# Sparse down of the second context token block on VectorE, in token-major form

## The chip, the cores and the metric

The kernel runs on 1 core of one Trainium2 chip, which has eight cores. The metric is the device time of one execution in microseconds; the median of the runs is compared. The five engines of the core that the text speaks of are PE (TensorE, products), DVE (VectorE), ACT (ScalarE), POOL (GpSimd, here the issuer of indirect gathers) and SP (SyncE, the issuer of all other transfers). They run side by side and each takes its instructions in the order in which they stand in its queue.

## The reference, cut to what matters

Two layers of a hybrid backbone run over 256 latent tokens (stream X) and 256 context tokens (stream C). Each layer ends with a PEER feed-forward: every token picks 128 experts (8 heads of 16) out of 16384, and each expert is one row of `u_emb` and one row of `v_emb`, 1024 numbers of 4 bytes each.

```
idx = ...                                    # (tokens, 8 heads, 16): the experts of each token
gate = softmax(best_s)
act = gelu(einsum('td,thkd->thk', h, u_emb[idx]))
out = einsum('thk,thkd->td', gate * act, v_emb[idx])     # 128 rows of v_emb, weighted and summed
ctx = ctx + g2c * out                        # in layer 0 alone; layer 1 leaves the context there
```

The change concerns the last sum, for the second 128 of the 256 context tokens in layer 0.

## The kernel before, in words

All 256 latent tokens take the feed-forward in a dense form (generator `dense`, lines 1149 to 1205): all 16384 experts are computed for all tokens and masked. The work goes in 64 steps (`i2`) of two blocks of 128 experts. A step has 48 products for the hidden side (helper `gemm`, lines 371 to 373, tile `pg`) and 48 for the output side (line 1199, tile `acc`). Its weights come as eight tiles `raw` of 256 KB (line 349, five buffers, issued on SP), and each is split into a high part on ACT (line 290, `wh`) and a low part on DVE (line 291, `wl`); a `raw` buffer is free when its low part is done. Two multiplications on DVE (line 1189, `ge`) apply the mask, which comes in tiles `gr` of 512 KB.

The 256 context tokens of layer 0 take it in a sparse form (generator `sparse`, lines 1007 to 1098), in two blocks of 128 tokens, `tb` 0 and 1. Three passes run over 128 positions each:

- `up(tb, p)` gathers, for slot p, one row of `u_emb` per token (tile `u`, 128 x 1024, 512 KB, one row on the partition of its token) and multiplies it with the token's activations `htok` on DVE, with a sum along the row (line 1038, two halves of 512).
- `mid(tb)` turns the sums into weights (gelu times gate) and transposes them on PE, so that each token has its 128 weights in one column `wT`.
- `down(tb, n)` takes one token t. It gathers the 128 rows of `v_emb` of that token (tile `v`, again 128 x 1024; the rows are the token's slots) and lets PE sum them over the partitions: the token's weight column is put into a small band of zeros `wz` (line 1057, once for four tokens), and two products of 32 x 512 (line 1065, each of which shows as two in the trace) add the token's row into the PSUM tiles `pf`.

Pass 0 has `up(0)`, pass 1 `down(0)` and `up(1)` in turns, and pass 2 `down(1)` alone. `fin(tb)` copies `pf` to a tile `f` (line 1071), transposes it by PE (line 1075) and adds it to the context stream (lines 1081 and 1084). Tiles `u`, `v` and `f` share one pool of four buffers of 512 KB, tag `g`.

A list written out by hand (`ORDER`, lines 1207 to 1216) cuts the generators of both streams into pieces, and a scheduler orders the instructions of each engine from it. Through pass 2 the dense steps of X run beside the context's `down(1)`. What comes behind `fin(1)` for the context is its part of layer 1 (a norm, line 314; products, line 367; a triangular solve on DVE, lines 736 and 738, whose results go to products of 32 x 32 at lines 760 and 771), which the latents of layer 1 need.

```
for a in range(3):
    for p in range(P):
        if a:
            down(a - 1, p)
        if a < 2:
            up(a, p)
...
```

Of the kernel before, what the change touches and what calls it, by code (L numbers as in the profile page):

```python
# [15 lines left out]
OP = mybir.AluOpType  # L16
# [153 lines left out]
class Kernel:  # L170
# [836 lines left out]
    def sparse(self, l, st, R):  # L1007
        hts, top = R["htok"], R["top"]
        nc, io, C, m = self.nc, self.io, self.C, self.M[l]
        V, A = nc.vector, nc.scalar  # L1010
        off = lambda ap: bass.IndirectOffsetOnAxis(ap=ap, axis=0)
        sp = self.S("sp", [P, 2, 4, P])
        for tb in range(2):
            ff = self.route(top, tb, "g")
            s, ef = sp[:, tb], self.S("ef", [P, P])
            V.scalar_tensor_tensor(ef.rearrange("p (h k) -> p h k", k=16), ff[:, 0], float(NK), ff[:, 1],
                                   op0=OP.mult, op1=OP.add)
            V.tensor_copy(s[:, 0].bitcast(I32), ef)
            pt = self.PS()
            nc.tensor.transpose(pt[:, :128], ef, C["ident"])  # L1020
            V.tensor_copy(s[:, 1].bitcast(I32), pt[:, :128])
            V.tensor_copy(s[:, 2].rearrange("p (h k) -> p h k", k=16), ff[:, 2])
            yield
        z = self.S("wz", [P, 512])
        nc.gpsimd.memset(z, 0.0)
        idx = lambda tb, i: sp[:, tb, i].bitcast(I32)
        pf = {}
        wT, d2 = [None, None], [None, None]

        def up(tb, p):  # L1030
            if p == 0 and self.DH[tb] == 2:
                d2[tb] = self.S("d2", [P, P])
            u = self.T4("u", tag="g")
            nc.gpsimd.indirect_dma_start(out=u, out_offset=None, in_=io["pu"], in_offset=off(idx(tb, 0)[:, p:p + 1]))  # L1034
            for k in range(self.DH[tb]):
                w = D // self.DH[tb]
                c = slice(w * k, w * k + w)
                V.scalar_tensor_tensor(u[:, c], u[:, c], 1.0, hts[tb][:, c], op0=OP.mult, op1=OP.mult,  # L1038
                                       accum_out=(sp[:, tb, 3] if k == 0 else d2[tb])[:, p:p + 1])

        def mid(tb):
            dots = sp[:, tb, 3]
            if self.DH[tb] == 2:
                V.tensor_tensor(dots, dots, d2[tb], op=OP.add)
            A.activation(dots, dots, AF.Gelu_apprx_tanh)
            V.tensor_tensor(dots, dots, sp[:, tb, 2], op=OP.mult)
            pt = self.PS()
            nc.tensor.transpose(pt[:, :128], dots, C["ident"])
            wT[tb] = self.S("ef", [P, P])
            V.tensor_copy(wT[tb], pt[:, :128])  # L1050
            pf[tb] = [self.PS("pf"), self.PS("pf")]

        def down(tb, n):
            j, g = n // 4, n % 4
            hz = z[:, 256 * (j % 2):256 * (j % 2) + 256]
            if g == 0:
                V.tensor_copy(hz.rearrange("p (g m) -> p g m", g=4)[:, :, 31],
                              wT[tb].rearrange("p (g j) -> p g j", g=4)[:, :, j])
            t = 32 * g + j
            o = 64 * g + 31 - j  # L1060
            v = self.T4("v", tag="g")
            nc.gpsimd.indirect_dma_start(out=v, out_offset=None, in_=io[f"pv{l}"], in_offset=off(idx(tb, 1)[:, t:t + 1]))  # L1062
            for hf in range(2):
                q = 32 * ((g + 2 * hf) % 4)
                nc.tensor.matmul(pf[tb][hf][q:q + 32], hz[:, o:o + 32], v[:, 512 * hf:512 * hf + 512],  # L1065
                                 start=j == 0, stop=j == 31)

        def fin(tb):
            f = self.T4("f", tag="g")
            for hf in range(2):  # L1070
                A.activation(f[:, 512 * hf:512 * hf + 512], pf[tb][hf], AF.Copy)
            for hf in range(2):
                pt = self.PS()
                for c in range(4):
                    nc.tensor.transpose(pt[:, 128 * c:128 * c + 128], f[:, 512 * hf + 128 * c:512 * hf + 128 * c + 128], C["ident"])
                for c in range(4):
                    v = self.xs[st][hf][:, c, 128 * tb:128 * tb + 128]
                    d = pt[:, 128 * c:128 * c + 128]
                    for q in range(2 if hf else 0):
                        i, o = slice(64 * (1 - q), 64 * (1 - q) + 64), slice(64 * q, 64 * q + 64)  # L1080
                        V.scalar_tensor_tensor(v[:, o], d[:, i], m["g2"][:, 4 * hf + c, st:st + 1], v[:, o],
                                               op0=OP.mult, op1=OP.add)
                    if hf == 0:
                        V.scalar_tensor_tensor(v, d, m["g2"][:, c, st:st + 1], v, op0=OP.mult, op1=OP.add)

        for a in range(3):
            for p in range(P):
# [4 lines that stand above are left out]
                if p % 8 == 7:  # L1092
                    yield
            if a:
                fin(a - 1)
            if a < 2:
                mid(a)
            yield
# [178 lines left out]
```

## Time and profile before

| what | value |
|---|---|
| median of 3 runs | 3490.35 us (3487.57 to 3492.45) |
| the profiled execution | 3496.04 us, of which its span is 3494.3 us |
| PE busy | 3315.0 us (95% of the span) |
| DVE, ACT, POOL busy | 2337.6, 1411.2, 553.1 us |
| granted TensorE clock, mean | 0.962 of full |
| bytes moved | 800.48 MB, mean 229 GB/s |
| `down(1)` and its `fin` | about 1620 to 2024 us of the span |

The profile comes from one execution on the chip. Busy time of PE counts pipelined products from start to modelled end, so 95% is not 95% of what PE could compute. "q0 software_dynamic" is the queue of POOL's gathers, "q1 hardware_dynamic" that of SP's transfers; both are served by the same 16 DMA engines.

### The profile page before, as it was taken

What the parts mean: (1) busy time and instruction counts of PE and PEld (TensorE: products, weight loads), DVE (VectorE), ACT (ScalarE), POOL (GpSimd) and SP (SyncE); (2) the same over time, 40 slices, a digit from 0 to 9 for tenths busy, and PEclk for the clock granted to TensorE, in tenths of its full rate; (3) what the DMA queues carried; (4) which work ended last, traced back from release to release, by engine and by line L of the source; (5) the groups of instructions that cost most, each with busy time, mean ns of one, the idle gap of its engine ahead of it and who ended that gap; (6) DMA issues with size and microseconds to landing.
All of it is one profiled execution on the core that took longest, in us unless ns stands there. A gap on an engine that the chain in (4) does not pass through costs nothing.

```text
span 3494.3 us, 69804 instructions
## 1 busy us (share of the span) xinstructions
PE 3315.0 (95%) x26540; PEld 2810.4 (80%) x26540; DVE 2337.6 (67%) x6304; ACT 1411.2 (40%) x2677; POOL 553.1 (16%) x529
## 2 busy tenths in 40 slices
PE   7999989799899879999999999899999999999999
PEld 4797668667667657777777799798889999999999
DVE  4864578777777976565333356877569998755555
ACT  3453133021113433333333354543545666455554
POOL 0000000444343434333333300000000000000000
PEclk9999989879999989999999999899999999999999
DMA  8534435789899999989888954332235567866654
GB/s 317 188 130 154 148 135 176 263 286 354 307 320 329 344 338 343 325 313 330 289 308 296 320 197 137 108 105 85 74 117 167 198 204 241 258 207 203 201 183 166
DMA packets 387297, 800.48 MB, mean 229 GB/s; under 512 B 36753, under 2 KB 105617, under 8 KB 386961
## 3 DMA queue, kind: packets, MB, share of 16 engines
q1 hardware_dynamic: 313232, 527.55, 44.7%
q0 software_dynamic: 73728, 268.47, 21.9%
q8 instruction: 209, 3.42, 0.4%
q14 instruction: 128, 1.04, 0.1%
HBM read 761.27 MB, written 34.60 MB: 228 GB/s over the span
## 4 chain that ended last, share of the span: by engine, by line
PE 51%; DMA 3%; DVE 2%; issue 2%; ACT 1%; POOL 0%; SPq 0%; DVEq 0%; POOLq 0%; ACTq 0%
PE acc L1199 16%; PE pg L371 8%; PE pg L373 8%; PE pg L372 7%; PE pf L1065 3%; PE pg L367 2%; PE ps L1141 2%; DMA gr<-gscr 1%; DMA u<-in_pu,sp 1%; PE ps L887 1%; DVE wl L291 0%; PE ps L400 0%; DMA raw<-in_pv 0%; PE ps L387 0%; ACT wh L290 0%
## 5 line engine op out<-in xcount | busy, mean ns | idle before, releaser
L291 DVE TENSOR_TENSOR wl<-raw,wh 128x512 fp32r<-128x512 f32 x1236 | 834.5, 688 | 451.4 <-ACT wh L290 419.8
L290 ACT ACTIVATE wh<-raw 128x512 fp32r<-128x512 f32 x1236 | 767.5, 629 | 867.3 <-PE pg L372 354.8
L371 PE MATMUL pg<-hi,wh 128*128 128x256 f32 x2768 | 810.8, 294 | 19.9 <-ACT hi L290 10.6
L373 PE MATMUL pg<-hi,wl 128*128 128x256 f32 x2768 | 797.5, 289 | 13.6 <-DVE wl L291 12.2
L372 PE MATMUL pg<-lo,wh 128*128 128x256 f32 x2768 | 800.1, 289 | 1.8 <-DVE lo L291 1.7
L371 PEld LDWEIGHTS pg<-hi,wh 128*128 128x128 f32 x2768 | 537.8, 195 | 90.9 <-issue 33.8
L1199 PE MATMUL acc<-wh,wh 128*128 128x256 f32 x2048 | 579.4, 289 | 13.0 <-ACT wh L290 12.5
L1199 PE MATMUL acc<-wl,wh 128*128 128x256 f32 x2048 | 572.0, 285 | 0.0
L373 PEld LDWEIGHTS pg<-hi,wl 128*128 128x128 f32 x2768 | 537.5, 195 | 26.0 <-DVE wl L291 14.9
L1199 PE MATMUL acc<-wh,wl 128*128 128x256 f32 x2048 | 543.9, 287 | 8.1 <-DVE wl L291 8.0
L372 PEld LDWEIGHTS pg<-lo,wh 128*128 128x128 f32 x2768 | 539.1, 195 | 12.8 <-issue 8.0
L1199 PEld LDWEIGHTS acc<-wh,wh 128*128 128x128 f32 x2048 | 395.1, 193 | 75.3 <-ACT wh L290 53.4
L1038 DVE SCALAR_TENSOR_TENSOR u<-u,htok 128x512 f32<-128x512 f32 x512 | 331.6, 685 | 116.0 <-DMA u<-in_pu,sp 110.6
L1199 PEld LDWEIGHTS acc<-wh,wl 128*128 128x128 f32 x2048 | 376.1, 193 | 38.1 <-DVE wl L291 19.9
L1199 PEld LDWEIGHTS acc<-wl,wh 128*128 128x128 f32 x2048 | 395.3, 193 | 8.4 <-issue 8.1
L1062 POOL DMA_INDIRECT v<-in_pv,sp x256 | 276.3, 1079 | 548.2 <-PE pf L1065 395.2
L367 PE MATMUL pg<-hf,raw 128*128 128x256 f32 x1488 | 350.6, 387 | 2.7 <-ACT hf L327 2.3
L367 PEld LDWEIGHTS pg<-hf,raw 128*128 128x128 f32 x1488 | 277.8, 193 | 62.7 <-issue 22.2
L1034 POOL DMA_INDIRECT u<-in_pu,sp x256 | 264.7, 1034 | 393.5 <-DVE u L1038 142.6
L1065 PE MATMUL pf<-v,wz 128*32 128x512 f32 x1024 | 253.3, 619 | 25.0 <-DMA v<-in_pv,sp 24.9
L1143 ACT ACTIVATE sg<-ps 128x256 f32<-128x256 f32 x256 | 135.7, 639 | 132.8 <-PE ps L1141 118.9
L1141 PEld LDWEIGHTS ps<-o,o 128*128 128x128 f32 x1024 | 135.2, 192 | 35.0 <-issue 19.8
(319 smaller groups left out, 3901.2 us busy)
## 6 DMA issues: line engine op xcount, KB each, us to landing
raw<-in_ut SPq DMA_DIRECT2D x512, 256.0 KB
raw<-in_pv SPq DMA_DIRECT2D x512, 256.0 KB
raw<-in_win SPq DMA_DIRECT2D x270, 256.0 KB
adaw<-in_ada SPq DMA_DIRECT2D x96, 512.0 KB
gscr<-sg SPq DMA_DIRECT2D x64, 512.0 KB
gr<-gscr SPq DMA_DIRECT2D x64, 512.0 KB
raw<-in_wq SPq DMA_DIRECT2D x96, 256.0 KB
raw<-in_wout SPq DMA_DIRECT2D x48, 256.0 KB
```

The costliest lines, as they stand in the source:

```text
L290: self.nc.scalar.activation(hi, src, AF.Copy)
L291: self.nc.vector.tensor_tensor(lo, src, hi.bitcast(F32), op=OP.subtract)
L367: nc.tensor.matmul(ps, raw[:, k - k0], act[k][2], start=k == 0, stop=k == K - 1)
L371: nc.tensor.matmul(ps, wh, hi, start=k == 0, stop=False)
L372: nc.tensor.matmul(ps, wh, lo, start=False, stop=False)
L373: nc.tensor.matmul(ps, wl, hi, start=False, stop=k == K - 1)
L1034: nc.gpsimd.indirect_dma_start(out=u, out_offset=None, in_=io["pu"], in_offset=off(idx(tb, 0)[:, p:p + 1]))
L1038: V.scalar_tensor_tensor(u[:, c], u[:, c], 1.0, hts[tb][:, c], op0=OP.mult, op1=OP.mult, accum_out=(sp[:, tb, 3] if k == 0 else d2[tb])[:, ...
L1062: nc.gpsimd.indirect_dma_start(out=v, out_offset=None, in_=io[f"pv{l}"], in_offset=off(idx(tb, 1)[:, t:t + 1]))
L1065: nc.tensor.matmul(pf[tb][hf][q:q + 32], hz[:, o:o + 32], v[:, 512 * hf:512 * hf + 512], start=j == 0, stop=j == 31)
L1141: nc.tensor.matmul(pg[:, 128 * u:128 * u + 128], o1[:, u], o2[:, u], start=True, stop=True)
L1199: nc.tensor.matmul(o, x, y[:, cs], start=i == 0 and n == 0 and c % 2 == 0, stop=i == NK - 1 and n == 2, skip_group_check=True)
```

## The change

For `tb` = 1 alone, `down` no longer takes one token but one slot: it gathers, for slot n, one row of `v_emb` per token (the same tile of 128 x 1024, indexed by the untransposed list `idx(tb, 0)`), and DVE multiplies it with the slot's weights, one per partition, and adds it to an accumulator of 128 x 1024. The accumulator is the block's activations tile `htok`, which `up(1)` no longer reads by then. `mid(1)` ends before its transpose, no `wz` columns are written and no `pf` tile is used; `fin(1)` transposes the accumulator directly and adds all eight pieces unrotated. `tb` = 0 is as before, and so is `ORDER`.

```diff
@@ mid
             V.tensor_tensor(dots, dots, sp[:, tb, 2], op=OP.mult)
+            if tb:
+                return
             pt = self.PS()
@@ down
         def down(tb, n):
+            if tb:
+                v, acc = self.T4("v", tag="g"), hts[tb]
+                nc.gpsimd.indirect_dma_start(out=v, out_offset=None, in_=io[f"pv{l}"], in_offset=off(idx(tb, 0)[:, n:n + 1]))
+                w = sp[:, tb, 3, n:n + 1]
+                if n == 0:
+                    V.tensor_scalar(acc, v, w, None, op0=OP.mult)
+                else:
+                    V.scalar_tensor_tensor(acc, v, w, acc, op0=OP.mult, op1=OP.add)
+                return
             j, g = n // 4, n % 4
@@ fin
-            f = self.T4("f", tag="g")
-            for hf in range(2):
+            f = hts[tb] if tb else self.T4("f", tag="g")
+            for hf in range(0 if tb else 2):
                 A.activation(f[:, 512 * hf:512 * hf + 512], pf[tb][hf], AF.Copy)
...
-                    for q in range(2 if hf else 0):
+                    rot = hf and not tb
+                    for q in range(2 if rot else 0):
...
-                    if hf == 0:
-                        V.scalar_tensor_tensor(v, d, m["g2"][:, c, st:st + 1], v, op0=OP.mult, op1=OP.add)
+                    if not rot:
+                        V.scalar_tensor_tensor(v, d, m["g2"][:, 4 * hf + c, st:st + 1], v, op0=OP.mult, op1=OP.add)
```

In the instruction order of DVE, amid pass 2, before the change (`wl` is the low part of a weight tile or of the masked hidden values, `ge` the mask multiplication, `wz` the copy of four tokens' weights):

```order
L1057 COPY wz_6660<-ef_10460 128x4
L291 TENSOR_TENSOR wl_18588<-raw_18586,wh_18587 128x512
L1189 TENSOR_TENSOR ge_18616<-ge_18616,gr_18461 128x2x128
L1189 TENSOR_TENSOR ge_18616<-ge_18616,gr_18463 128x2x128
L291 TENSOR_TENSOR wl_18626<-raw_18624,wh_18625 128x512
L291 TENSOR_TENSOR wl_18632<-raw_18630,wh_18631 128x512
L291 TENSOR_TENSOR wl_18773<-ge_18616,wh_18772 128x512
L291 TENSOR_TENSOR wl_18662<-raw_18660,wh_18661 128x512
```

and at the same place with the change (line 1063 is the new accumulation, L1201 the former L1189):

```order
L1063 SCALAR_TENSOR_TENSOR htok_4907<-v_10743,sp_6269,htok_4907 128x1024
L291 TENSOR_TENSOR wl_18180<-raw_18178,wh_18179 128x512
L291 TENSOR_TENSOR wl_18186<-raw_18184,wh_18185 128x512
L1063 SCALAR_TENSOR_TENSOR htok_4907<-v_10746,sp_6269,htok_4907 128x1024
L291 TENSOR_TENSOR wl_18217<-raw_18215,wh_18216 128x512
L291 TENSOR_TENSOR wl_18223<-raw_18221,wh_18222 128x512
L1201 TENSOR_TENSOR ge_18134<-ge_18134,gr_18288 128x2x128
L1201 TENSOR_TENSOR ge_18134<-ge_18134,gr_18290 128x2x128
L291 TENSOR_TENSOR wl_18295<-ge_18134,wh_18294 128x512
L1063 SCALAR_TENSOR_TENSOR htok_4907<-v_10749,sp_6269,htok_4907 128x1024
```

What moved: a 128 x 1024 operation that needs a gathered tile now stands between nearly every one or two low parts, 128 of them in all, in one queue with them.

On PE, amid pass 2, before the change (the hidden side of a dense step, with the products of two tokens in it):

```order
L373 MATMUL pg_19001<-hi_8270,wl_19040 128x256
L1065 MATMUL pf_10462<-v_10961,wz_6660 32x512
L1065 MATMUL pf_10463<-v_10961,wz_6660 32x512
L1065 MATMUL pf_10462<-v_10965,wz_6660 32x512
L1065 MATMUL pf_10463<-v_10965,wz_6660 32x512
L371 MATMUL pg_19001<-hi_8280,wh_19045 128x256
L372 MATMUL pg_19001<-lo_8281,wh_19045 128x256
L1199 MATMUL acc_12446<-wh_19081,wh_19086 128x256
```

and at the same place of a dense step with the change:

```order
L373 MATMUL pg_18523<-hi_8270,wl_18562 128x256
L371 MATMUL pg_18523<-hi_8280,wh_18567 128x256
L372 MATMUL pg_18523<-lo_8281,wh_18567 128x256
L1211 MATMUL acc_12273<-wh_18599,wh_18604 128x256
L1211 MATMUL acc_12273<-wl_18600,wh_18604 128x256
```

What moved: the 256 products of pass 2 are gone from PE. Counted over PE's whole queue, 1104 products of line 1199 stand between the transposes of `fin(0)` and those of `fin(1)` before the change, which is 23.0 dense steps, and 1036 with it, which is 21.6. The triangular solve of the context's layer 1 and its products of 32 x 32 (line 760) stood behind the last dense step before; they now stand at step 63 of 64, ahead of its end. POOL's queue has the same gathers at the same places.

## Rows read from the trace of the kernel before

**Rows 1.** The page, busy time of the engines, then 40 slices.
```profile
PE 3315.0 (95%) x26540; PEld 2810.4 (80%) x26540; DVE 2337.6 (67%) x6304; ACT 1411.2 (40%) x2677; POOL 553.1 (16%) x529
...
DMA  8534435789899999989888954332235567866654
```
**Rows 2.** Windows: stretch, us, busy (instructions) by engine, granted clock, DMA share, GB/s.
```profile
627.00:905.00 278.00, 243.81 (x1669) 192.35 (x1669) 213.38 (x658) 44.71 (x99) 126.58 (x126) 0.86 0.88 309
1165.00:1620.00 455.00, 403.51 (x2745) 313.43 (x2745) 308.44 (x774) 164.93 (x289) 177.37 (x165) 0.95 0.95 333
1620.00:2024.00 404.00, 401.11 (x2737) 289.07 (x2737) 159.68 (x304) 138.05 (x236) 134.05 (x127) 1.00 0.88 304
2024.00:2220.00 196.00, 196.00 (x1540) 182.34 (x1539) 130.00 (x303) 95.64 (x182) 2.86 (x3) 0.97 0.45 151
2220.00:2250.00 30.00, 19.80 (x226) 18.73 (x225) 23.83 (x61) 16.67 (x32) 0.00 (x0) 0.64 0.23 71
```
**Rows 3.** Groups of instructions by line, 1620 to 2024.
```profile
L1062 POOL DMA_INDIRECT v<-in_pv,sp x127 | 134.0, 1055 | 262.9 <-PE pf L1065 253.3 <-issue 6.7 <-DMA v<-in_pv,sp 1.4
L291 DVE TENSOR_TENSOR wl<-raw,wh 128x512 fp32r<-128x512 f32 x186 | 122.2, 688 | 83.3 <-ACT wh L290 71.7 <-issue 5.5 <-PE pf L1065 2.3
L1189 DVE TENSOR_TENSOR ge<-ge,gr 128x256 f32<-128x256 f32 x46 | 17.9, 421 | 43.2 <-ACT ge L1165 24.4 <-issue 13.4 <-DMA gr<-gscr 5.4
L291 DVE TENSOR_TENSOR wl<-ge,wh 128x512 fp32r<-128x512 f32 x23 | 16.0, 695 | 11.3 <-ACT wh L290 9.8 <-issue 1.5
```
**Rows 4.** The chain of waits, 1620 to 2024, by line.
```profile
by line: PE acc L1199 35.1%; PE pf L1065 26.5%; PE pg L371 12.8%; PE pg L373 11.1%; PE pg L372 10.9%; ACT wh L290 1.4%; issue 1.0%; DVE wl L291 0.7%; DVE ge L1189 0.2%; ACT ge L1165 0.2%; ACT f L1071 0.2%; PE ps L1048 0.0%; DVE wz L1057 0.0
```
**Rows 5.** Timeline of PE, 1806 to 1808: start, us, instruction.
```profile
1806.73 0.28 PE L1199 MATMUL acc<-wl,wh 128*128 128x256 f32 x1
1806.85 0.28 PE L1199 MATMUL acc<-wh,wl 128*128 128x256 f32 x1
1807.06 1.05 PE L1065 MATMUL pf<-v,wz 128*32 128x512 f32 x4
1808.05 0.38 PE L1199 MATMUL acc<-wh,wh 128*128 128x256 f32 x1
```
**Rows 6.** DMA, 1620 to 2024: queue, packets, MB, share of 16 engines' time.
```profile
DMA packets 57801, 122.72 MB, mean 304 GB/s; under 512 B 5229, under 2 KB 17517, under 8 KB 57768
...
q0 software_dynamic: 18423, 67.08, 47.3%
q1 hardware_dynamic: 39345, 55.20, 40.2%
```
**Rows 7.** DMA, 627 to 905 (pass 0, gathers of `u` alone).
```profile
q0 software_dynamic: 17938, 65.34, 66.9%
```
**Rows 8.** Waits: 1620 to 2024 (first), 1620 to 2024 of SP's queue, 1165 to 1620.
```profile
POOL v L1062 <- PE pf L1065: 253.3, 99, 7.5
...
SPq L349 <- DVE wl L291: 249.4, 151, 8.2
...
DVE u L1038 <- DMA u<-in_pu,sp: 50.9, 24, 5.7
```
**Rows 9.** Sources of lines 779 and 1038: duration ns min/median/max.
```profile
L779 DVE TENSOR_TENSOR tu<-TF,ge x8: 1204/1222/1226, 218.7 to 2480.8; 128x1024 f32<-128x1024 f32 x8
L1038 DVE SCALAR_TENSOR_TENSOR u<-u,htok x512: 639/685/743, 627.7 to 1619.8; 128x512 f32<-128x512 f32 x171
```
**Rows 10.** Windows of 20 to 100 us, columns as in Rows 2.
```profile
650.00:700.00 50.00, 33.97 (x462) 30.36 (x464) 40.04 (x130) 3.61 (x9) 25.40 (x26) 0.79 0.87 300
1100.00:1150.00 50.00, 50.00 (x266) 37.60 (x265) 42.27 (x167) 17.70 (x32) 16.29 (x15) 1.00 0.97 340
1190.00:1240.00 50.00, 37.41 (x216) 24.09 (x216) 49.11 (x157) 22.46 (x45) 22.96 (x21) 0.97 0.96 342
1240.00:1260.00 20.00, 6.60 (x16) 1.40 (x16) 8.39 (x25) 2.35 (x5) 6.98 (x8) 0.54 0.99 341
```

## The prediction

> **What bounds the kernel now.** I read the page first: PE is busy 95% of the span, POOL 16%, DVE 67%, and the slices show DMA at eight or nine tenths through the middle third [rows 1]. An average over the span says nothing of pass 2, so I went to the windows. From 1620 to 2024, the stretch of the second block's down, PE is busy 401.1 of 404 us at full clock, DVE only 160, POOL 134, and DMA 88% at 304 GB/s [rows 2]. The chain of waits for the same stretch is PE from end to end: 35.1% and 34.8% lie on the two sides of the dense steps and 26.5% on line 1065, the products that go away [rows 4]. Who waits confirms it: POOL's gathers stand 253.3 of 404 us for a buffer that PE still reads, while gathers that PE or DVE would wait for hardly show [rows 3, 8]. So before the change pass 2 ends when PE is through, and DMA has a reserve, but a small one: 12%. In pass 1, where every position has two gathers, DMA is at 95% and 333 GB/s over 455 us and PE falls to 403.5 of 455 [rows 2]. That stretch is my model for what comes next.
>
> **What goes from PE.** Dense products start every 0.12 us (1806.73, 1806.85 [rows 5]), so a step of 96 takes 11.5 us. Between the two `fin` stand 23.0 steps, 265 us; 404 less 3 idle less 265 leaves 136 us for 128 tokens, 1.06 each. One token in the timeline agrees: 1806.85 to 1808.05 is 1.20, less 0.12 [rows 5]. With the change 21.6 steps stand there, 249 us of PE, and the other 1.4 steps (16 us) come behind `fin`, where PE is busy 196 of 196 us [rows 2] and every microsecond moved there is paid.
>
> **What comes to DVE.** 128 accumulations of 128 x 1024. No row shows a scalar_tensor_tensor of that size. The nearest is the two-input multiplication of line 779, 1.22 us; the same operation at half width takes 0.685 (without its accumulator read), so two halves, 1.37, are the upper end [rows 9]. I take 1.22, as two of 512 pay the fixed part twice: 156 us, at most 175. The dense work of a step is (122.2 + 17.9 + 16.0) / 23 = 6.8 us [rows 3], 147 us for 21.6 steps. Sum 303 us (up to 322). The 32 copies of `wz`, the two copies of `pf` and one transpose go; all were beside other work, I count nothing for them.
>
> **What stays on POOL and the queues.** The 128 gathers keep their place in POOL's queue: 128 x 1.055 = 135 us [rows 3], far below the rest. Does a row per token and slot cost DMA more than a token's 128 rows? Pass 0 gathers slot-wise: 65.34 MB in 66.9% of 278 us, 351 GB/s of engine time [rows 7]; pass 2 gathers token-wise: 67.08 MB in 47.3% of 404 us, also 351 [rows 6]. No difference. SP's loads wait 249.4 us for DVE to free a `raw` [rows 8]; the new accumulations stand in that same queue, so this is the wait to watch.
>
> **What DMA needs.** Gathers 0.473 x 404 = 191 us. SP's transfers 0.402 x 404 = 162 us for 23 steps, 152 for 21.6 [rows 6]. Together 343 us if all 16 engines never pause.
>
> **The sum.** For the work up to `fin(1)`: PE 249, DVE 303 plus its waits, POOL 135, DMA 343. DMA becomes the longest. It never ran at 100% over a long stretch: pass 1 reached 95%, pass 0 and pass 2 88% [rows 2]. So 343 / 0.95 = 361 us, with ends 343 (share 1.00) and 390 (share 0.88). I take 0.95, because that is the stretch where gathers and `raw` loads both press. Add the 16 us of moved steps: 377 against 404, **27 us less** (ends: 45 less, 2 more). About 109 of the 136 us taken from PE turn into waits for data.
>
> [...]
>
> Behind the dense steps: from 2220 to 2250 PE idles 10 us at a mean clock of 0.64 [rows 2]. The context's solve now stands ahead of the end of the dense steps, so its products could fill this; but the latents' own norm stands there too and is not shortened. Bound 0 to 10 us less; I take 0. The rest of the span keeps its work.
>
> The profiled execution took 3496.04 us, 5.7 above the median of the three runs. I apply the difference to the median: 3490.35 - 27 = **3463 us**.
>
> **The rivals.**
>
> *DMA has no more to give.* PE's products were covering gathers that could not come faster; the share stays at 0.88. For it: pass 0 has DVE and PE both unfilled and 0.88 [rows 2]. Against: pass 1 and the window 1100 to 1150, at 0.97 with PE full [rows 10]; and in pass 2 the gathers waited for PE, not PE for gathers [rows 3]. Time: 390 + 16 = 406, 2 more: 3492, no change.
>
> *DVE's queue becomes the bound (slower).* One queue now holds the accumulations, which wait for gathers, and the low parts, which free SP's buffers and feed PE; a late gather delays both. In pass 1 DVE waited 50.9 us for gathers in 82 positions [rows 8], 0.62 each; 128 such waits are 79 us, and 303 + 79 = 382, still no loss. But over pass 1 DVE was busy only 308 of 455 us, 68% [rows 2]. If that is all such a coupled queue can do, the stretch takes 303 / 0.68 = 446, plus 16: 58 more, **3548**. The turn is at 77%: below it, 303 / 0.77 + 16 is over 404 by 5 us, and more. Against: DVE at 42.3 of 50 and 49.1 of 50 in windows with DMA at 0.97 and 0.96 [rows 10], and 213 of 278, just 77%, in pass 0 [rows 2].
>
> *PE's clock falls.* PE drops from 99% busy to 249 of 361, 69%, in many short pieces. In the windows the clock is 0.97 where PE was busy 37 of 50 us, but 0.79 where it was 34 of 50, and 0.54 where it was 6.6 of 20 after waiting for gathers [rows 10]. [...]
>
> *Better than the sum.* The share goes to 1.00 and the gap at 2220 closes: 45 + 10 = 55 less, 3435.
>
> *It doesn't do what it says.* The products of pass 2 would still be issued. The order shows them gone from PE's queue, so this has no chance of its own.
>
> **How the numbers follow.** About 0.2% (7 us) is what a measurement of this kernel can tell from no change. Forecast, DMA-bound, 8 to 45 us less: 0.58. Better: 0.06. Share stays at 0.88, within 7 us: 0.16. DVE's queue, over 7 us slower: 0.13. The clock: 0.07. Faster 0.58 + 0.06 = 0.64, same 0.16, slower 0.13 + 0.07 = 0.20. The forecast's own range is 3445 to 3483. For 8 in 10 it is widened to 3440, which takes in half of the gap, and up to 3505, which takes in the unchanged case and DVE's queue down to a share of about 75%; what lies above (most of the two slower cases, some 0.14) and below (0.05) is left out.
>
> **What would show it.** Right: no line for products into `pf` after about 1620; the window from there to `fin(1)` some 361 us long, PE at 65 to 75% busy, DVE at 80 to 88%, DMA at 0.93 or more and 325 GB/s or more; PE's idle time ended by `wh` and `wl`, and behind them by `raw` and `v` landing; POOL's wait moved from PE to DVE's accumulation, which takes 1.2 to 1.4 us; behind it PE full again, the clock in the stretch above 0.9. Wrong: the stretch at 390 us or more with DMA at 0.88 (the first rival), DVE's idle time ended by gathers while landed `raw` tiles wait (the second), the granted clock below 0.7 with PE full (the third), or the time returned behind `fin(1)`, where then something other than PE must end last.

## The result, and the profile after

The changed kernel takes **3452.18 us** (median of 4 runs, 3444.63 to 3453.53) against 3491.24 for the kernel before on the same chip: ratio **0.9882**, 95% interval 0.9869 to 0.9895, 39 us less. The forecast was 3463. The profiled execution took 3452.36 us with a span of 3450.6, where before it was 3496.04 and 3494.3.

The page of the changed kernel, the busy line and the slices of DMA (before: [rows 1]):

```profile
PE 3221.8 (93%) x26027; PEld 2811.0 (81%) x26027; DVE 2481.1 (72%) x6395; ACT 1413.1 (41%) x2675; POOL 575.8 (17%) x529
...
DMA  8444435789999999999999953332235667866654
```

PE lost 93 us and DVE gained 143. The slices at nine tenths now run without a break through what was pass 2. The windows of the changed kernel, columns as in [rows 2], cut at the first transposes of `fin(0)` and `fin(1)` (1627.2 and 1977.1 us) and at the end of the dense product (2203.3):

```profile
1627.20:1977.10 349.90, 289.00 (x2076) 271.15 (x2077) 292.87 (x379) 130.92 (x220) 156.63 (x127) 0.92 0.95 336
1977.10:2203.30 226.20, 221.27 (x1986) 207.56 (x1984) 156.94 (x358) 116.39 (x216) 2.86 (x3) 0.98 0.47 159
2203.30:2250.00 46.70, 46.50 (x467) 44.30 (x467) 30.55 (x84) 24.42 (x51) 0.00 (x0) 0.89 0.29 101
```

The kernel before at the same cuts ([rows 2] has its pass 2 cut at 1620 and 2024):

```profile
1621.70:2025.40 403.70, 401.49 (x2743) 290.36 (x2744) 159.21 (x302) 138.77 (x238) 133.65 (x127) 1.00 0.88 303
2025.40:2225.80 200.40, 200.40 (x1574) 186.50 (x1572) 135.73 (x316) 96.80 (x184) 2.86 (x3) 0.97 0.46 153
2225.80:2270.00 44.20, 32.14 (x519) 30.27 (x518) 34.13 (x86) 30.05 (x57) 0.00 (x0) 0.73 0.24 80
```

From these the 43.7 us of span split up: up to `fin(0)` +5.5 (1621.7 to 1627.2, the same order); **pass 2 -53.8** (403.7 to 349.9); from `fin(1)` to the end of the dense product **+25.8** (200.4 to 226.2); from there to the end **-21.2** (1268.5 to 1247.3). The last rows of both lists show where more than half of the 21 lie: PE stood still for 12 of 44.2 us behind the dense product, and now for 0.2 of 46.7.

The groups of the changed kernel in 1627 to 1977 (before: [rows 3]), and its waits there (before: [rows 8]):

```profile
L1063 DVE SCALAR_TENSOR_TENSOR htok<-v,sp,htok 128x1024 f32<-128x1024 f32 x127 | 162.3, 1278 | 14.3 <-DMA v<-in_pv,sp 13.6
L1058 POOL DMA_INDIRECT v<-in_pv,sp x127 | 157.0, 1236 | 188.3 <-DVE htok L1063 165.8 <-DMA v<-in_pv,sp 7.7 <-DVE htok L1061 4.3
L291 DVE TENSOR_TENSOR wl<-raw,wh 128x512 fp32r<-128x512 f32 x174 | 114.9, 683 | 9.3 <-ACT wh L290 9.1
```
```profile
ACT wh L290 <- DMA raw<-in_ut: 53.5, 44, 4.7
...
ACT wh L290 <- DMA raw<-in_pv: 36.1, 27, 3.3
```

The products into `pf` are gone. POOL waits for DVE's sum in place of PE (165.8 us); DVE waits 13.6 us for gathers, ACT 89.6 us for `raw` (53.5 and 36.1), and behind ACT stands PE, which waits 31.4 us for `wh` (24.9 at line 371, 6.5 at line 1211). DMA in the same stretch (before: [rows 6]):

```profile
DMA packets 54091, 117.50 MB, mean 336 GB/s; under 512 B 4945, under 2 KB 15898, under 8 KB 54062
...
q0 software_dynamic: 18320, 66.69, 52.9%
q1 hardware_dynamic: 35742, 50.44, 41.4%
```

### The profile page after: what moved, and what is told of

It reads as the page before. It is cut to its first block, busy times and chain, and to the rows that moved or that the text cites. A ratio compares the mean times of both kernels' runs of the same rounds, so it can differ in the third digit from the quotient of the medians.

```text
span 3450.6 us, 68996 instructions
## 1 busy us (share of the span) xinstructions
PE 3221.8 (93%) x26027; PEld 2811.0 (81%) x26027; DVE 2481.1 (72%) x6395; ACT 1413.1 (41%) x2675; POOL 575.8 (17%) x529
## 3 DMA queue, kind: packets, MB, share of 16 engines
q14 instruction: 128, 1.05, 0.1%
## 5 line engine op out<-in xcount | busy, mean ns | idle before, releaser
L373 PE MATMUL pg<-hi,wl 128*128 128x256 f32 x2768 | 808.6, 293 | 27.6 <-DVE wl L291 25.4
L371 PEld LDWEIGHTS pg<-hi,wh 128*128 128x128 f32 x2768 | 545.1, 197 | 79.6 <-ACT wh L290 41.2
L373 PEld LDWEIGHTS pg<-hi,wl 128*128 128x128 f32 x2768 | 544.6, 197 | 44.0 <-DVE wl L291 37.9
L1211 PE MATMUL acc<-wh,wl 128*128 128x256 f32 x2048 | 544.6, 288 | 21.9 <-DVE wl L291 21.2
L1058 POOL DMA_INDIRECT v<-in_pv,sp x128 | 158.1, 1235 | 191.4 <-DVE htok L1063 165.8
L1073 POOL DMA_INDIRECT v<-in_pv,sp x128 | 140.2, 1095 | 280.5 <-PE pf L1076 143.6
L1063 DVE SCALAR_TENSOR_TENSOR htok<-v,sp,htok 128x1024 f32<-128x1024 f32 x127 | 162.3, 1278 | 14.3 <-DMA v<-in_pv,sp 13.6
```

The costliest lines, as they stand in the source:

```text
L371: nc.tensor.matmul(ps, wh, hi, start=k == 0, stop=False)
L373: nc.tensor.matmul(ps, wl, hi, start=False, stop=k == K - 1)
L1063: V.scalar_tensor_tensor(acc, v, w, acc, op0=OP.mult, op1=OP.add)
L1211: nc.tensor.matmul(o, x, y[:, cs], start=i == 0 and n == 0 and c % 2 == 0, stop=i == NK - 1 and n == 2, skip_group_check=True)
```

## The experiments

The theory is that pass 2 was bound by PE and is bound by DMA now. The rivals are that VectorE's queue or the four buffers bound it, and that the gap behind the dense product closed by chance. All runs stand in one table. A step is 96 dense products; "solve" is the dense step beside which the context's solve stands in PE's order; the last column, "rest", is the span less the first transpose of `fin(1)`.

| kernel | ratio to before (95%) | steps in pass 2 | pass 2, us | GB/s | steps behind | solve at | rest, us |
|---|---|---|---|---|---|---|---|
| before | 1 | 23.0 | 403.7 | 303 | 11.0 | 64.0 | 1468.9 |
| the change | 0.9882 (0.9869 to 0.9895) | 21.6 | 349.9 | 336 | 12.4 | 63.0 | 1473.5 |
| change_again | 0.9869 (0.9853 to 0.9886) | 21.6 | 349.6 | 336 | 12.4 | 63.0 | 1474.0 |
| pe_back | 1.0050 (1.0033 to 1.0068) | 24.0 | 420.6 | 294 | 10.0 | 64.0 | 1465.0 |
| half_sum | 0.9826 (0.9789 to 0.9863) | 20.0 | 324.9 | 352 | 14.0 | 62.2 | 1491.3 |
| half_rows | 0.9681 (0.9652 to 0.9711) | 22.0 | 277.9 | 306 | 12.0 | 64.0 | 1482.4 |
| extra_bytes | 1.0044 (1.0027 to 1.0061) | 21.6 | 345.2 | 340 | 12.4 | 64.0 | 1482.9 |
| extra_in_pass | 0.9974 (0.9958 to 0.9990) | 24.8 | 404.0 | 350 | 9.2 | 64.0 | 1455.6 |
| no_extra | 0.9918 (0.9899 to 0.9936) | 25.0 | 395.5 | 316 | 9.0 | 64.0 | 1452.1 |
| extra_burst | 1.0036 (1.0016 to 1.0056) | 20.8 | 396.2 | 334 | 13.2 | 62.2 | 1483.5 |
| block0_only | 1.0025 (1.0009 to 1.0041) | 24.2 | 430.1 | 293 | 12.2 | 63.8 | 1481.3 |
| both_blocks | 0.9933 (0.9913 to 0.9952) | 21.4 | 358.7 | 330 | 15.0 | 60.2 | 1504.4 |
| order_only | 0.9905 (0.9874 to 0.9936) | 21.5 | 350.1 | 333 | 13.0 | 62.2 | 1484.1 |
| five_buffers | 0.9884 (0.9851 to 0.9917) | 16.6 | 305.0 | 349 | 24.4 | 51.1 | 1630.4 |

**PE put back.**

```diff
                     V.scalar_tensor_tensor(acc, v, w, acc, op0=OP.mult, op1=OP.add)
+                if n == 0:
+                    pf[1] = [self.PS("pf"), self.PS("pf")]
+                for hf in range(2):
+                    q = 32 * ((n % 4 + 2 * hf) % 4)
+                    nc.tensor.matmul(pf[1][hf][q:q + 32], z[:, 0:32], v[:, 512 * hf:512 * hf + 512],
+                                     start=n < 4, stop=n >= P - 4)
                 return
```

> The change with 256 products on TensorE put back into the second block's slot loop: 32 columns of the zero tile against each of the two halves of every gathered tile, into two PSUM tiles that nobody reads. VectorE still makes the sum. Theory (the pass between the two blocks' transposes was bound by TensorE before, 404 us, and by DMA now, 350 us): in the order of this kernel 24.0 steps of the dense product lie between the two transposes (21.6 in the change, 23.0 in the kernel before), so TensorE needs 24.0 x 11.5 = 276 plus the 136 of the products = 412 us, with TensorE over 97% busy and the DMA share falling to about .85; behind it fewer steps are left, so the whole run comes near the kernel before (ratio to it 0.995 to 1.01). Rival (the products cost no path time, the gain came from gathers that are issued slot-wise or from buffers freed by VectorE): the pass is bound by bytes, 67.1 MB + 24.0 x 2.34 MB = 123 MB at 336 GB/s = 367 us, and the run stays near the change (ratio about 0.985 to 0.99).

The window of pass 2 of pe_back, the first of its waits there, and its chain of waits by line (before: [rows 4]):

```profile
1626.30:2046.90 420.60, 420.05 (x2802) 299.08 (x2803) 310.89 (x406) 142.73 (x244) 156.57 (x127) 1.00 0.88 294
```
```profile
POOL v L1058 <- PE pf L1068: 170.1, 75, 4.6
```
```profile
by line: PE acc L1217 35.9%; PE pf L1068 29.0%; PE pg L373 12.0%; PE pg L371 11.7%; PE pg L372 11.0%; ACT wh L290 0.4%; ACT f L1088 0.1%; issue 0.0%
```

The pass took 420.6 us with PE busy for all but 0.6 of them; 412 was expected, 367 by the rival. With the products back, PE is the bound: the chain lies on PE from end to end, DMA's share falls to 0.88 as before, and POOL waits for PE. The sum hides beside it, in a VectorE that is busy 311 us of the stretch in all. The run ends 18 us of span above the kernel before: its pass is 17 us longer, of which the one step more in it accounts for 11.5, it starts 5 us later, and the step that left the rest gave only 4 us back there.

**Half the sum, then half the rows.**

```diff
-                    V.scalar_tensor_tensor(acc, v, w, acc, op0=OP.mult, op1=OP.add)
+                    V.scalar_tensor_tensor(acc[:, :512], v[:, :512], w, acc[:, :512], op0=OP.mult, op1=OP.add)
```
half_rows besides:
```diff
+    a["ph"] = np.ascontiguousarray(g["peer_v"][0][:, :512])
...
-                nc.gpsimd.indirect_dma_start(out=v, out_offset=None, in_=io[f"pv{l}"], ...
+                nc.gpsimd.indirect_dma_start(out=v[:, :512], out_offset=None, in_=io["ph"], ...
```

> The change with the sum on VectorE made over 512 of the 1024 columns only (the other half of the result is left out); every row is still gathered whole. Theory (DMA bounds the pass): the order of this kernel has 20.0 steps of the dense product in the pass, so 67.1 + 20.0 x 2.34 = 113.9 MB at 336 GB/s = 339 us; VectorE's busy time in the pass falls by about 127 x 0.64 = 81 us and its share to some 60%, and the pass moves only by the 11 us of the bytes; the 1.6 steps that now lie behind it cost 18 us there, so the run is from 5 us faster to 15 us slower than the change (ratio to before 0.986 to 0.993). Rival (VectorE's queue bounds the pass at its 84% busy): the pass falls with VectorE's work, to between 262 and 290 us, and the run is 30 to 60 us faster than the change (ratio 0.97 to 0.98). Also asked: whether a gather's issue on GpSimd, 1.24 us in the change against 1.06 before, comes back down when VectorE reads its two operands for half as long: if the two share something, the mean falls to 1.10 to 1.17 us; if it is the order of the table of slots, it stays at 1.24.

> As half_sum (VectorE sums 512 of 1024 columns, the other half of the result is left out), and each slot's gather brings only these 512 columns, from a table of half the width: 33.6 MB less. VectorE's work is the same as in half_sum, so the difference of the two is the bytes alone. The order has 22.0 dense steps in the pass. Theory (DMA bounds the change's pass): 33.6 + 22.0 x 2.34 = 85 MB at 336 GB/s = 253 us, and TensorE needs 22.0 x 11.5 = 253 us: both at the limit, the pass takes 255 to 275 us with TensorE over 92% busy. The run is 70 to 90 us faster than the change (ratio to before 0.96 to 0.97), less up to 20 us if the gap behind the dense product opens again. Rival (a chain of fixed latency through four buffers, issue to landing to sum, bounds it; or VectorE): with the packets as many and VectorE as in half_sum, the pass stays within 25 us of half_sum's.

half_rows narrows the first slot's multiplication in the same way. Pass 2 of half_sum, then of half_rows, each with its chain of waits:

```profile
1621.50:1946.40 324.90, 267.34 (x1953) 251.07 (x1953) 223.14 (x365) 123.17 (x205) 143.96 (x127) 0.92 0.98 352
by line: DMA v<-in_pv,sp 28.9%; issue 21.6%; DMA raw<-in_ut 11.7%; DMA raw<-in_pv 7.9%; POOL v L1058 6.6%; DVE wl L291 5.0%; DMA gr<-gscr 4.6%; DVE htok L1063 3.5%; PE acc L1211 2.1%; PE pg L373 1.7%; ACT wh L290 1.5%; PE pg L371 1.3%; DVE 
```
```profile
1628.30:1906.20 277.90, 263.37 (x2101) 259.80 (x2102) 229.28 (x383) 132.10 (x222) 152.17 (x127) 0.97 0.92 306
by line: PE acc L1212 25.8%; DMA raw<-in_pv 12.3%; issue 9.4%; DMA gr<-gscr 7.5%; PE pg L374 7.1%; PE pg L372 6.9%; PE pg L373 6.9%; DMA raw<-in_ut 6.8%; ACT wh L291 5.0%; DVE wl L292 3.9%; DVE htok L1064 2.8%; DMA v<-in_ph,sp 2.3%; SPq L35
```

Taking 70 us of work off DVE shortened the pass by 25 us, between the theory's 11 and the rival's 60 and more. Of the 25, 9 are bytes (114.5 MB where the change has 117.5, at 336 GB/s); 16 are a rate that rose from 336 to 352 GB/s and a share from 0.95 to 0.98. So the sum on VectorE may hold DMA back, by up to 16 us of 350. This is not shown, as the order changed with it: half_sum has 1.6 steps fewer in the pass, and both passes took 16.2 us per step (324.9 / 20.0 and 349.9 / 21.6). With the same sum and half-width rows the pass fell by 47 us more, though 2.0 more dense steps stand in it, to 12.6 us per step and 95% busy on PE: the bytes were what held half_sum. The chains say the same: gathers landing (`v`) are 28.9% of half_sum's and 2.3% of half_rows'. A chain of fixed latency through four buffers and a fixed time per dense step, which the narrow rows leave as they were, are excluded as the bound there.

**More bytes.** Three placements of 32 copies of 512 KB, DRAM to DRAM. extra_bytes:

```diff
+        scr = self.dr.tile([32, P, 1024], F32, tag="scr", name=self.nm("scr"))
...
+                if n % 4 == 0:
+                    nc.sync.dma_start(scr[n // 4], io["pv0"][128 * n:128 * n + 128])
```
extra_in_pass, in place of the last two lines (no_extra is this without its last two lines):
```diff
+                if n % 4 == 0:
+                    nc.sync.dma_start(scr[n // 4, 0:1, 0:1], v[0:1, 0:1])
+                if n % 4 == 3:
+                    nc.sync.dma_start(scr[n // 4], io["pv0"][128 * n:128 * n + 128])
```
extra_burst, extra_bytes with this ahead of the copies:
```diff
+                if n == 0:
+                    nc.sync.dma_start(scr[:, 0, 0:1], sp[0:32, tb, 3, 0:1])
```

> The change with 32 more transfers on SyncE's queue, one for every fourth slot of the second block, each a plain copy of 512 KB from the table in DRAM to a scratch tensor in DRAM that nobody reads; the steps of the dense product between the transposes are 21.58, as in the change. Theory (DMA bounds the pass, nothing else is near): 16.8 MB more at 336 GB/s lengthen the pass by 50 us, to 400, and the run by 45 to 55 us (ratio to before 1.002 to 1.005); TensorE and VectorE are as busy in us as in the change. Rival (VectorE's queue or the latency of four buffers bounds it, and DMA at .95 is only nearly full): the pass takes some of it into the 5% that is free, 17 us, and the run is 10 to 30 us slower than the change.

The copies of extra_bytes on SP's queue (count, issue ns min/median/max, first and last start), and its pass 2:

```profile
L1062 SPq DMA_DIRECT2D scr<-in_pv x32: 488/488/593, 15.8 to 66.6; - x32
```
```profile
1675.50:2020.70 345.20, 282.73 (x2086) 265.51 (x2087) 293.72 (x379) 130.59 (x220) 163.74 (x127) 0.95 0.96 340
```

It missed its question: the copies wait for nothing, so the order put them at the very start of the program, 15.8 to 66.6 us into the span. They cost their time there: the first gather starts at 674.7 us where the change's starts at 624.2, and `fin(0)` comes 48 us later (1675.5 for 1627.2). The run says nothing of what bounds pass 1 or pass 2. It became a control for something else: pass 2 and the count of steps behind it are as in the change, only the solve stands at 64.0, and the rest is 9.4 us longer than the change's.

> As extra_bytes, whose 32 copies of 512 KB were all placed ahead of the second pass: each copy now waits for a 4-byte write from the slot's gathered tile to the same scratch rows, so that it runs in the pass, one for every fourth slot. The order of this kernel has 24.8 dense steps in the pass (21.6 in the change). Theory (DMA bounds the pass): 67.1 + 24.8 x 2.34 + 16.8 = 142 MB at 336 GB/s = 423 us, with the DMA share at .93 or more and TensorE near 286 of them busy (68%). Rival (VectorE's queue bounds the pass at its 84% share): 24.8 steps bring VectorE to 314 us, so the pass takes 314 / .84 = 374 us and the share stays near .95 with GB/s above 370.

> extra_in_pass without its copies; only the 32 writes of 4 bytes stay, which make the order put 25.0 dense steps into the second pass (21.6 in the change, 24.8 in extra_in_pass, where the pass took 404.0 us). Bytes theory: 67.1 + 25.0 x 2.34 = 125.6 MB at 340 GB/s (336 in the change, 350 in extra_in_pass) = 369 us, 35 us less than extra_in_pass for 16.4 MB less, with TensorE 25 x 11.5 + some 45 us of other work = 330 us busy, 89%. Behind it 9.0 dense steps are left: 182 us to the end of the dense product as in extra_in_pass (9.2) and 1274 behind that, since the context's solve then stands at the very end. Sum: 1623 + 369 + 180 + 1274 = 3446 us of span, 5 us less than the change (ratio to before 0.984 to 0.990), so that the steps moved forward win some 40 us in the dense product and lose most of it in the work behind it that they covered. Rival 1 (VectorE's queue bounds the pass): 25.0 steps give it 315 us, at 84% 375 us; with the extra bytes of extra_in_pass then hidden, this pass would be as long as that one, 395 to 405 us. Rival 2 (the work behind is not bound by its cover): the tail stays at 1249 and the run is 30 us faster than the change (ratio 0.980).

> The change itself, unaltered, on the same chip as no_extra: 0.987 to 0.9895 of the kernel before; its second pass 345 to 355 us.

> The change with the same 32 copies of 512 KB, all behind one small write at the second block's first slot: they go out as one burst on SyncE's queue at the start of the pass, and the order stays near the change's, 20.8 dense steps in the pass (21.6). Bytes theory (in the change's order DMA is the bound): 67.1 + 20.8 x 2.34 + 16.8 = 132.6 MB at 336 to 350 GB/s = 379 to 395 us. Rival (queues and buffers coupled: what no_extra and extra_in_pass showed, where 16.4 MB cost 8.5 us): 20.8 steps take 338 to 345 us as in the change, and the copies add 10 us or less, 345 to 355 us. Between the two, 355 to 379, DMA and the sum on VectorE share the pass.

change_again repeats the change: 0.9869 and a pass of 349.6 us. Pass 2 of extra_in_pass, of no_extra with its chain, and of extra_burst, with its longest wait for `raw` and the 58 us behind its burst:

```profile
1618.60:2022.60 404.00, 331.43 (x2376) 312.96 (x2377) 316.76 (x416) 151.90 (x253) 154.11 (x127) 0.92 0.97 350
```
```profile
1624.80:2020.30 395.50, 327.25 (x2387) 310.15 (x2388) 314.64 (x416) 150.47 (x254) 158.88 (x127) 0.94 0.91 316
by line: DMA v<-in_pv,sp 31.6%; issue 19.9%; DMA gr<-gscr 6.5%; DVE htok L1066 5.5%; DVE wl L291 5.4%; PE acc L1214 4.5%; DMA raw<-in_ut 4.3%; DMA raw<-in_pv 4.0%; PE pg L373 3.3%; POOL v L1059 3.1%; ACT wh L290 2.9%; PE pg L371 2.4%; PE pg
```
```profile
1619.10:2015.30 396.20, 276.04 (x1992) 258.86 (x1993) 290.70 (x372) 125.44 (x212) 153.69 (x127) 0.87 0.94 334
```
```profile
ACT wh L290 <- DMA raw<-in_pv: 97.1, 32, 58.1
```
```profile
1639.00:1697.00 58.00, 0.00 (x0) 0.00 (x0) 8.99 (x7) 0.60 (x1) 6.58 (x7) 0.52 1.00 347
```

The three do not say the same. In extra_burst, whose order is nearest the change's, the copies cost their full price: 396.2 us, where 20.8 steps at the change's rate would take 345 (67.1 + 48.7 MB at 336 GB/s). One wait of 58.1 us stands behind the burst, and nothing later made up for it. But in these 58 us PE did no product and DVE was busy for 9. A pass that is bound by DVE's queue or by the buffers could not have made up such a standstill either. So extra_burst shows a pass without slack and does not tell the bounds apart. In extra_in_pass the rate rose to 350 and the pass came to 404 us, 19 less than the theory's 423. And no_extra, without the copies, took 395.5 us where 369 was expected: 16.4 MB less saved 8.5 us, and DMA had 9% to spare. So at 25 steps in the pass, in that order, bytes alone are not the bound; DVE is busy 314.6 of 395.5 us, 80%. The chain of no_extra lies on gathers landing for 31.6% and on issue for 19.9%, and on the sum itself for 5.5%: a gather waits for a free buffer, is issued, lands and is summed before its buffer can be used again. Whether this round is held by DVE's queue, by the small writes that read every fourth gathered tile, or by the order that was laid out around them, no run separates. That bytes bind rests on half_rows, with half the sum; for the change's own pass it is argued from there and from its share of 0.95. Bytes, sum and the four buffers together hold it, and their parts are not shown.

**The other block, and both.**

```diff
-            if tb:
+            if not tb:
                 return
...
-            if tb:
+            if not tb:
                 v, acc = self.T4("v", tag="g"), hts[tb]
```
and the same turn in `fin`; both_blocks drops the condition.

> The same edit on the first block instead of the second: its down part is summed on VectorE from slot-wise gathers, the second block's goes over TensorE as before. The pass ahead of the first transposes already has both gathers of 128 slots and a DMA share of .95 with TensorE 89% and VectorE 68% busy. Theory (what counts is which engine bounds the pass; this one was bound by DMA): nothing is gained by taking 2 x 128 products off TensorE there, and VectorE gets 157 us more on top of 309, less 2.4 dense steps that the order takes out of the pass (15 us): 451 us, so it becomes a second bound. The pass (457 us from 1165 before) takes 445 to 480 us though 2.4 dense steps are gone from it (17 us of bytes); the second pass is bound by TensorE as before, 24.2 x 11.5 + 136 = 415 us. The run is 10 to 40 us slower than before (ratio 1.003 to 1.012). Rival (products on TensorE cost path time wherever they are): the first pass gets 30 to 60 us shorter and the run 20 to 45 us faster than before.

> Both blocks' down parts summed on VectorE from slot-wise gathers; no products of the sparse part are left on TensorE. Theory: the first pass is bound by VectorE and DMA together as in block0_only, 445 to 480 us with 2.4 dense steps fewer; the second by DMA, 21.4 steps, 350 us; the 2.6 steps more that lie behind it cost 30 us there. The run is 20 to 50 us slower than the change (ratio to before 0.994 to 1.003). Rival (TensorE's work is what the run is made of, 93% busy): another 136 us taken off TensorE make the run 30 to 50 us faster than the change.

Pass 1 from the first gather of `down(0)` to 1165 in the kernel before and in block0_only, then from 1165 to `fin(0)` in block0_only and in both_blocks:

```profile
907.00:1165.00 258.00, 247.31 (x1251) 181.20 (x1250) 202.52 (x830) 62.50 (x127) 98.79 (x93) 0.99 0.91 320
902.00:1165.00 263.00, 208.31 (x1127) 184.49 (x1125) 258.76 (x868) 65.67 (x131) 112.76 (x99) 0.92 0.95 337
1165.00:1582.70 417.70, 317.69 (x2112) 294.14 (x2112) 376.63 (x795) 149.38 (x259) 184.22 (x158) 0.83 0.94 330
```
```profile
1165.00:1592.30 427.30, 315.57 (x2112) 293.46 (x2113) 385.22 (x811) 149.58 (x259) 183.20 (x163) 0.82 0.94 329
```

Both sizes were missed, the ranking held. From 1165 on DVE stands at 90% and the rate stays at 330 GB/s, against 333 of the kernel before with its products on PE [rows 2]. Ahead of 1165 DVE did become a bound: it is busy 258.8 of 263 us there, beside a DMA share of 0.95, where before PE was busy 247 of 258 us. `fin(0)` comes 39 us sooner all the same (1582.7 against 1621.7), for 2.4 steps that left the pass; they stand later, where PE is full. Over the whole run block0_only ends 9 us above before and, by the ratios, both_blocks 18 us above the change. In a pass where DMA already held 0.95 for most of the time, taking work off PE bought nothing for the run: PE is 76% busy there.

**The order alone.**

```diff
-... Xd.22:x^60 Cmi ...
+... Xd.22:x^-1200 Cmi ...
```

> The change with one number of the table that sets the order moved (the dense product's 22 steps behind the sparse stage get the priority -1200 in place of 60), the same instructions otherwise: 21.5 dense steps in the second pass as in the change, the passes half a step earlier, and the context's solve at dense step 62.2 (63.0 in the change, 64.0 in the kernel before). It prices what the order alone is worth. Theory (about 10 of the change's 44 us come from the gap behind the dense product, which closes when the solve stands one step or more ahead of its end): the second pass takes 350 us, the rest behind the dense product 1249 to 1258, and the run is within 8 us of the change (ratio to before 0.986 to 0.990). Rival (the gap's closing was chance): the rest behind the dense product takes 1266 to 1271 us as before, and the run is 15 to 20 us slower than the change.

Pass 2 took 350.1 us as expected; by the ratios the run is 8 us above the change, and its interval (0.9874 to 0.9936) takes in the change's 0.9882. Behind the dense product it took 1249 us, at the near end of the theory's 1249 to 1258.

**A fifth buffer**, the one attempt at a faster kernel.

```diff
-    N4 = {"m": 15, "dl": 12, "g": 4}
-    N1 = {"m": 6, "l": 5}
+    N4 = {"m": 15, "dl": 12, "g": 5}
+    N1 = {"m": 5, "l": 5}
...
-    NT2, NRAW, NWP = 6, 5, 4
+    NT2, NRAW, NWP = 5, 5, 4
```

> The change with five buffers for gathered rows instead of four (paid for with one of six 512-column and one of six 256-column tiles elsewhere). The order moves far: the first block's transposes stand at dense step 23.0 (30.0), the second's at 39.6 (51.6), so 16.6 dense steps lie in the pass and the context's chain starts 12 dense steps sooner. Bytes theory: the first pass has 7 x 2.34 = 16.4 MB less, 1165 to 1575; the second 67.1 + 16.6 x 2.34 = 106 MB at 340 GB/s = 312 us; TensorE idles there 83 and 76 us instead of 52 and 61, and nothing is gained behind, where TensorE is the bound: the run is 10 to 40 us slower than the change, less up to 20 for a context chain that is never waited for. Rival (the hold of four buffers through landing and sum is what kept the share at .95): with a fifth the passes move 350 GB/s or more at a share of .98, the second takes 303 us or less, and the run is 10 to 30 us faster than the change.

Windows of five_buffers, pass 1, pass 2 and the dense steps behind:

```profile
1165.00:1522.60 357.60, 313.24 (x2025) 231.76 (x2023) 250.91 (x649) 123.24 (x220) 158.13 (x144) 0.94 0.97 345
1522.60:1827.60 305.00, 234.15 (x1621) 217.71 (x1621) 262.88 (x327) 101.83 (x172) 161.91 (x126) 0.90 0.97 349
1827.60:2212.60 385.00, 384.42 (x3450) 368.09 (x3451) 247.82 (x510) 193.01 (x343) 2.86 (x3) 0.98 0.53 170
```

The rival came nearer on the rate: the passes move 345 and 349 GB/s at 0.97, against 333 [rows 2] and 336 at 0.95, which speaks for the hold of four buffers as a part of what kept the share at 0.95, though the order moved with it. The run is not faster than the change all the same (0.9884), and not slower as the theory had it. The gathers ran ahead of the dense product, and 24.4 dense steps now stand behind `fin(1)`, 385 us with PE full. No kernel here that computes the whole result beats the change.

## Why the prediction was right, point by point

**Pass 2.** The step "PE 249, DVE 303 plus its waits, POOL 135, DMA 343; DMA becomes the longest" held in the main, with 350 us for 361. The share was taken as 0.95 and is 0.95. That it came out so exactly is in part luck: no run derives this share, and passes with the whole sum and four buffers that PE did not bound stood anywhere from 0.91 (no_extra) to 0.97 (extra_in_pass). The miss of 11 us lies in the term under it: gathers at "191 us" took 0.529 x 350 = 185, SP's transfers at "152" took 0.414 x 350 = 145, so 330 for 343: in engine time the gathers moved 360 GB/s (66.69 MB in 185 us) where the prediction had 351 from [rows 6]. The share is not DMA's alone: with half the sum it rose to 0.98, with a fifth buffer to 0.97. At 84% busy DVE was 7 points above the turn of the rival "DVE's queue becomes the bound"; no_extra, at 80% and with DMA at 0.91, shows that this rival is not far away.

No pass here came above 352 GB/s, and that one had half the sum; the change at 336 was near the 333 of the stretch of pass 1 that the prediction took [rows 2].

**DVE.** The accumulation was taken at 1.22 us from line 779, with 1.37 as the upper end; it takes 1.278, 127 times 0.058 = 7 us more. All of DVE came to 293 us against 303. The window counts time once where two operations overlap; added up by groups, as the prediction did, it is 308 (162.3, 114.9, 16.4 and 14.4).

**PE.** "65 to 75% busy" was wrong: 289 of 350 is 83%. The removed part was right (pe_back brings it back), but a dense product took 139 ns (289.0 / 2076) in place of 120. The granted clock of 0.92 is part of it: from 1730 to 1736 us it was 0.50, and dense products started 0.21 us apart there (1734.54, 1734.75), where from 1850 to 1856, at 1.00, they start 0.12 apart (1850.14, 1850.26). No run separates the rest. It stayed hidden. The rival "PE's clock falls" did not come: 0.92 in the pass at 83% busy, and not below 0.82 in any pass whose window stands here, even at 74% (both_blocks, 315.57 of 427.3 us). What a pass at the low clock throughout would take, no run shows; the chance of 0.07 was the author's estimate.

**The moved steps.** "16 us" for 1.4 steps is right in the controls. With 11.5 us a step, the rest of 1468.9 of before becomes 1480.4 for half_rows, 1485.2 for extra_bytes, 1482.6 for block0_only; measured 1482.4, 1482.9, 1481.3. In these the solve stands at the end, as before.

**The gap.** "Bound 0 to 10 us less; I take 0": it gave 11.7 (1473.5 for 1485.2), a little over the bound. In every kernel whose solve stands 1 to 4 dense steps ahead of the end, the rest is shorter than by steps: half_sum by 12, both_blocks 10, extra_burst 10, order_only 8 (five_buffers, 13 steps ahead, is not: 7 longer). The timeline of PE behind the last dense product, before and after:

```profile
2225.57 0.28 PE L1199 MATMUL acc<-wh,wl 128*128 128x256 f32 x1
2226.39 1.02 PE L314 MATMUL ps<-ones,sq 128*128 128x1 f32 x8 [0.55 <-ACT sq L312]
```
```profile
2203.07 0.28 PE L1211 MATMUL acc<-wh,wl 128*128 128x256 f32 x1
2203.28 2.08 PE L788 MATMUL ps<-tu,kt 64*64 64x64 f32 x64
2205.29 5.07 PE L314 MATMUL ps<-ones,sq 128*128 128x1 f32 x32
```

PE now goes on with products of the context, and the squares of the norm are ready when it is through. This is an effect of the order that the change brought along, not of its own work: extra_bytes has the change's steps without it and is 9.4 us longer there. The prediction saw the cause and priced it at nothing.

**The sum.** Forecast -27: pass -43, moved steps +16, gap 0. Measured -43.7 of span: pass -53.8, moved steps +16.3, gap -11.7, and +5.5 up to `fin(0)`, where the order is the same. So the pass gave 11 us more than forecast and the gap 12 more, and the 5.5 us took a part of that back; they are spread, as runs with the same order so far have `fin(0)` anywhere from 1618.6 (extra_in_pass) to 1628.3 (half_rows).

**What stays open:** how the bound of the change's pass divides between bytes, sum and buffers; the bound of no_extra's pass; and why fewer than 11 steps behind `fin(1)` give less than 11.5 us each back (pe_back, extra_in_pass and no_extra are 6 to 8 us longer than by steps), for which the lost cover of the context's chain is only the likely reason.

## What to carry to other kernels

Work taken off the engine that ended last was worth, here, no more than the distance to the next resource in that stage: pass 2 gave 54 us of the 61 between PE's 404 and DMA's 343. So sum up each resource's need for the stage, and take the share it reached where it was already the bound (0.95 here). In the stage that was bound by transfers for most of its time the same edit was worth nothing to the run (block0_only, 1.0025 of before). The edit also moved other work in the scheduler's order (1.4 dense steps, 16 us): count it per step, and look at what stands at the next seam.

## What the runs showed of the hardware that was not expected

Issuing a gather took POOL 1.055 us before [rows 3] and 1.236 in the change. Over the 127 gathers of each pass, the timeline gives one answer in both. Where no operation of DVE with two input tiles runs as a gather's issue starts, or begins within 0.3 us, it takes 0.94 us, and none is longer than 1.0: 51 gathers before, 11 in the change. Where one does, most are longer: 41 of 76 before, 105 of 116 in the change. One of them, on POOL and on DVE:

```profile
1814.91 1.86 POOL L1058 DMA_INDIRECT v<-in_pv,sp  x1 [1.86 <-DVE htok L1063]
```
```profile
1813.37 2.59 DVE L1063 SCALAR_TENSOR_TENSOR htok<-v,sp,htok 128x1024 f32<-128x1024 f32 x2
```

The issue begins 1.05 us before the second accumulation ends (1815.96) and ends 0.81 us behind it. So the trace has POOL's issue longer beside such operations of DVE. DVE's accumulation is not longer beside an issue: 77 of them begin while an issue runs, and they take 1.267 to 1.286 us like the other 50. What joins the two was not shown. half_sum had asked this too: with accumulations half as long, the mean fell to 1.136 us, inside the 1.10 to 1.17 expected if the two share something; half_rows, with accumulations of the same length, stood at 1.201, and change_again at 1.283 where the change has 1.236, so the fall is shown only roughly. No run took the overlap away by itself. It cost nothing here, as POOL waited 165.8 us for buffers anyway.
